# SSM layer of a two-layer decoder trunk: u exchanged inside SBUF, one order of loads for tables and GLU weights, gelu's table loaded earlier, gemvs moved out of the last stages, four gating buffers

## The chip, the cores and the metric

The kernel runs on one core of one Trainium2 chip. The core has a matrix engine (TensorE, PE in the profile), a vector engine (VectorE, DVE), a scalar engine (ScalarE, ACT), a general engine (GpSimd, POOL), a synchronisation engine (SyncE, SP) that here issues most DMAs, and 16 DMA engines that all queues share. Each engine works through its own list of instructions in order; an instruction waits until the semaphores it names have reached their values. The metric is the device time of one execution in microseconds (us).

## The reference

The whole computation is a decoder trunk of two layers on one sequence of 512 tokens and 1024 channels, all in float32. Layer 0 mixes tokens by stick-breaking attention, layer 1 by a complex diagonal state-space model (SSM) with a gated linear unit; a gated feed-forward layer with a short causal convolution follows each. The change is in the SSM:

```python
def s5_ssm(h, w_in, a_re, a_im, log_dt, b_re, b_im, c_re, c_im, d_skip, w_glu, b_glu, w_o):
    b, s, d = h.shape
    u = h @ w_in
    ug = u.reshape(b, s, N_GROUPS, SSM_GROUP)            # 64 groups of 16 channels
    lam = lax.complex(a_re, a_im)
    dt = jnp.exp(log_dt)[:, None]
    lam_bar = jnp.exp(lam * dt)
    b_bar = ((lam_bar - 1) / lam)[..., None] * lax.complex(b_re, b_im)
    bu = jnp.einsum('gph,bsgh->bsgp', b_bar, ug)
    # states: x[t] = lam_bar * x[t-1] + bu[t], 64 complex states for each group
    _, states = lax.associative_scan(combine, (a_seq, bu), axis=1)
    y = jnp.einsum('ghp,bsgp->bsgh', c_mat, states).real.reshape(b, s, d)
    z = jax.nn.gelu(y + d_skip * u)
    g = z * jax.nn.sigmoid(z @ w_glu + b_glu)
    return g @ w_o
```

## The kernel before

Tokens lie along the free axis and channels along the 128 partitions, so x is eight tiles of 128x512. A product of float32 values is made of three matmuls (`mm3`, L167): each operand is split into a rounded part (h) and a remainder (l), and TensorE adds hh, hl and lh. A weight is loaded by SP into a raw buffer, ScalarE makes the h part, DVE the l part (`load_w`, L145).

The SSM layer works on eight blocks of 128 channels. The 512 tokens are 64 chunks of 8. For block bi:

- `u_out` (L1149): the product u = h w_in is copied from PSUM by ScalarE into `ut` (two buffers), reordered by place in the chunk. ScalarE's queue writes it to DRAM (`sU`, L1153), SP's queue reads it back (L1155) in the form that the scan needs: a partition holds one of a group's 16 channels at one of the 8 places in the chunk. `u` has four buffers.
- `st_scan` (L1168): TensorE makes `pv` from u and table `pB`; DVE rotates it with table `pR`, scans over the 64 chunks (L1192) and rotates back; ScalarE copies the states into `st`. ScalarE first copies the decay rates into `rho` (L1172).
- `st_out` (L1205): TensorE makes `py`, first sixteen matmuls of u with table `pT` (inside a chunk), then sixteen of `st` with table `pC` (from the chunks before); ScalarE copies it to `yn`.
- `st_tr` (L1217): four transposes by TensorE into `pz`, then ScalarE's gelu gives z (L1223). Gelu lies in another function table of ScalarE than what ran before it, so an ACT_TABLE_LOAD stands ahead of its first use.
- `glu_units`, `glu_w` (L1239, L1246): z times the GLU weights. Five of the eight output tiles are accumulated block by block (weights `wglk`), the other three at the end (weights `wgl`). Sigmoid, the gating product and its split follow (L1298 to L1305), into `sg`, `gzH`, `gzL`; then the out-projection (weights `wos`) adds to x, tile by tile.

The loop over s_ from 2 to 9 (L1261) runs these as a pipeline: in stage s_ stand py of block s_-2, pv of block s_, some dense matmuls, pz of block s_-2 and more dense matmuls. The tables B, R, T and C of every block were computed earlier and lie in DRAM (`sB`, `sR`, `sT`, `sC`); each has two buffers in SBUF, and its load for block bi waits until block bi-2 has read its own.

TensorE's order is written out (`pe_pin`, pinned matmuls); a scheduler orders the rest by its own estimate. `follow("P", ...)` chains DMAs on SP's queue in program order. `behind_head` keeps work behind given instructions.

The gemvs (`gemv_step`, L191) are single steps of adaLN's modulation: a 512 KB tile of `w_modT` is loaded by SP into `wg` (two buffers) and reduced by DVE in one instruction (L196). `bg(n)` puts the next n of them at a place in the program.

Every DMA that SP or ScalarE issues signals its end on one of eight completion counters (DMAHW0 to DMAHW7 below; POOL's are DMASW0 to DMASW7). They are dealt out in turn over both queues, and a DMA that takes a counter waits until the DMA that had it last has landed.

## Time and profile before

| | before |
|---|---|
| time, median of 3 runs | 1194.81 us (1194.74 to 1198.65) |
| time of the profiled execution | 1194.65 us |
| its span | 1192.7 us |
| mean clock granted to TensorE | 0.991 |
| SSM layer in the span, roughly | 640 to 830 us |
| DMA, hardware queue of SP (q1) | 83026 packets, 205.76 MB, 53.9% of 16 engines |
| DMA, hardware queue of ScalarE (q10) | 8320 packets, 2.10 MB, 0.8% |
| DMA, software queue of POOL (q0) | 576 packets, 2.10 MB, 0.5% |

The span is the time from the first to the last instruction in the profile. A row of a timeline gives start and duration in us, the engine (SPq and ACTq are DMAs being issued by SP and ScalarE), the line, the operation, what it writes <- what it reads, and how often it stands in a row (x2). In brackets stands how long the engine had been idle before it, and what ended that. In the chain of waits a row is start, duration, and what the time went to. A row of a window lists its length and then, for PE, PEld, DVE, ACT and POOL, the busy time and the number of instructions, and at the end the clock, the share of the DMA engines and GB/s. A row of waits gives the line, what it waited for, the sum in us, how often, and the longest.

### The profile page before, as it was taken

To read this page: it belongs to the slowest core of one execution; us is meant where nothing else is said; L and a number is where in the kernel's file an instruction comes from. 1 tells how busy PE (TensorE), PEld (TensorE's weight loads), DVE (VectorE), ACT (ScalarE), POOL (GpSimd) and SP (SyncE) were. 2 spreads that over 40 slices of the span, in tenths; PEclk is the share of its full clock that TensorE was granted. 3 is DMA by queue.
4 is the path that set the end of the run, shared out by engine and by line. 5 is a ranking of instruction groups with operands and counts; after the bars stand their busy time and mean duration, and the time that the engine had idled before them with its cause. 6 is when DMAs were issued, how large, how long until landed. Compare 5 with 4: busy or idle time off the path is not lost.

```text
span 1192.7 us, 16459 instructions
## 1 busy us (share of the span) xinstructions
PE 1168.8 (98%) x6218; PEld 964.4 (81%) x6218; DVE 885.8 (74%) x1312; ACT 563.7 (47%) x893; POOL 270.4 (23%) x245
## 2 busy tenths in 40 slices
PE   8999999999999999989999999999999999999997
PEld 6887677699787878768889887879888888888887
DVE  6978988565999489888868598787598467744555
ACT  6756667456443134413336577646554134422443
POOL 1000000000298899998710000000000000000003
PEclk8999999999999999989999999999999999999999
DMA  8875653231348567778755598762166437442222
GB/s 301 316 262 165 203 179 109 90 121 54 89 142 273 177 215 222 207 233 294 247 153 182 182 322 288 246 224 77 53 216 225 124 118 188 153 124 71 83 76 71
DMA packets 92002, 211.00 MB, mean 177 GB/s; under 512 B 19602, under 2 KB 37906, under 8 KB 91923
## 3 DMA queue, kind: packets, MB, share of 16 engines
q1 hardware_dynamic: 83026, 205.76, 53.9%
q10 hardware_dynamic: 8320, 2.10, 0.8%
q0 software_dynamic: 576, 2.10, 0.5%
q8 instruction: 48, 0.79, 0.3%
q14 instruction: 32, 0.25, 0.1%
HBM read 188.68 MB, written 21.24 MB: 176 GB/s over the span
## 4 chain that ended last, share of the span: by engine, by line
PE 70%; POOL 8%; DVE 8%; DMA 7%; ACT 3%; issue 2%; SPq 1%; POOLq 0%; ACTq 0%; DVEq 0%
PE up L169 9%; PE up L172 9%; PE up L173 9%; PE dn L172 5%; PE dn L169 5%; PE dn L173 5%; PE o L772 2%; DVE ca L459 1%; PE t L754 1%; PE k L169 1%; PE q L169 1%; PE wo L169 1%; PE q L172 1%; PE q L173 1%; PE wo L173 1%
## 5 line engine op out<-in xcount | busy, mean ns | idle before, releaser
L173 PE MATMUL up<-hH,up_l 128*128 128x512 f32 x640 | 249.3, 390 | 1.1 <-DVE up_l L164 1.1
L169 PE MATMUL up<-hH,up_h 128*128 128x512 f32 x640 | 249.5, 390 | 0.0
L172 PE MATMUL up<-hL,up_h 128*128 128x512 f32 x640 | 249.3, 390 | 0.0
L459 DVE SCALAR_TENSOR_TENSOR ca<-up,small,ca 128x511 f32<-128x511 f32 (+1 forms) x176 | 131.4, 746 | 84.2 <-ACT ca L457 81.4
L196 DVE SCALAR_TENSOR_TENSOR wg<-wg,cact 128x1024 f32<-128x1024 f32 x96 | 122.8, 1294 | 40.1 <-DMA wg<-in_w_modT_dram 39.9
L172 PE MATMUL dn<-gL,dn_h 128*128 128x512 f32 (+1 forms) x394 | 145.9, 370 | 3.4 <-DVE gL L474 3.4
L169 PE MATMUL dn<-gH,dn_h 128*128 128x512 f32 (+1 forms) x394 | 146.3, 372 | 2.1 <-ACT gH L473 2.1
L173 PE MATMUL dn<-gH,dn_l 128*128 128x512 f32 (+1 forms) x394 | 145.7, 370 | 0.0
L173 PEld LDWEIGHTS up<-hH,up_l 128*128 128x128 f32 x640 | 120.1, 188 | 26.9 <-DVE up_l L164 2.0
L169 PEld LDWEIGHTS up<-hH,up_h 128*128 128x128 f32 x640 | 120.1, 188 | 26.0 <-issue 1.2
L172 PEld LDWEIGHTS up<-hL,up_h 128*128 128x128 f32 x640 | 120.1, 188 | 24.4
L1368 POOL TENSOR_SCALAR xa<-x,Anorm_out 128x256 f32<-128x256 f32 x7 | 5.7, 815 | 573.7 <-ACT dn_h L163 558.9
L163 ACT ACTIVATE up_h<-up_r 128x1024 fp32r<-128x1024 f32 x80 | 84.2, 1053 | 104.7 <-PE dn L172 48.0
L164 DVE TENSOR_TENSOR up_l<-up_r,up_h 128x1024 fp32r<-128x1024 f32 x80 | 121.9, 1524 | 10.1 <-ACT up_h L163 9.2
L457 ACT ACTIVATE ca<-up,small 128x512 f32<-128x512 f32 x88 | 67.7, 770 | 90.3 <-PE up L173 90.3
L172 PEld LDWEIGHTS dn<-gL,dn_h 128*128 128x128 f32 x394 | 75.1, 191 | 16.3 <-DVE gL L474 4.0
L169 PEld LDWEIGHTS dn<-gH,dn_h 128*128 128x128 f32 x394 | 75.0, 190 | 15.9 <-ACT gH L473 3.0
L173 PEld LDWEIGHTS dn<-gH,dn_l 128*128 128x128 f32 x394 | 75.0, 190 | 12.4
L353 DVE SCALAR_TENSOR_TENSOR x<-dn,mod,x 128x512 f32<-128x512 f32 (+1 forms) x55 | 37.3, 679 | 61.6 <-PE dn L173 61.6
L163 ACT ACTIVATE dn_h<-dn_r 128x1024 fp32r<-128x1024 f32 (+1 forms) x48 | 46.7, 981 | 55.9 <-PE dn L172 28.0
L466 ACT ACTIVATE ca<-ca 128x512 f32<-128x512 f32 x44 | 27.8, 632 | 91.7 <-DVE ca L459 89.9
L164 DVE TENSOR_TENSOR dn_l<-dn_r,dn_h 128x1024 fp32r<-128x1024 f32 (+1 forms) x48 | 62.8, 1308 | 8.3 <-ACT dn_h L163 8.1
(324 smaller groups left out, 2352.2 us busy)
## 6 DMA issues: line engine op xcount, KB each, us to landing
wg<-in_w_modT_dram SPq DMA_DIRECT2D x96, 512.0 KB
up_r<-in_w_up_dram SPq DMA_DIRECT2D x80, 512.0 KB
dn_r<-in_w_down_dram SPq DMA_DIRECT2D x32, 512.0 KB
wgs<-in_w_modT_dram SPq DMA_DIRECT2D x16, 512.0 KB
dn_r<-in_w_down_dram SPq DMA_DIRECT2D x16, 384.0 KB
wv_r<-in_w_v_dram SPq DMA_DIRECT2D x8, 512.0 KB
wk_r<-in_w_qk_dram SPq DMA_DIRECT2D x8, 512.0 KB
wq_r<-in_w_qk_dram SPq DMA_DIRECT2D x8, 512.0 KB
```

Source lines behind the costliest of these rows:

```text
L163: order("S", lambda: S.activation(wh[:, :n], raw[:, :n], AF.Copy))
L164: pin["split"] = order("V", lambda: V.tensor_tensor(wl[:, :n], raw[:, :n], wh[:, :n].bitcast(F32), ALU.subtract))
L169: ins = PE.matmul(ps, ah, bh, start=start, stop=False)
L172: PE.matmul(ps, ah, bl, start=False, stop=False)
L173: PE.matmul(ps, al, bh, start=False, stop=stop)
L196: mul = lambda: V.scalar_tensor_tensor(w, w, 1.0, cact, ALU.mult, ALU.mult, accum_out=raw[:, col:col + 1])
L353: add = lambda: V.scalar_tensor_tensor(xs, pv, gate, xs, ALU.mult, ALU.add)
L457: follow("S", lambda: S.activation(ca, ps, AF.Identity, bias=small[:, cb:cb + 1], scale=tapw[2]))
L459: follow("V", lambda: V.scalar_tensor_tensor(ca[:, q:], ps[:, :T - q], tapw[2 - q], ca[:, q:], ALU.mult, ALU.add))
L466: follow("S", lambda: S.activation(cg, cg, AF.Silu))
L754: ins = PE.transpose(pt[:, c:c + P], wts[pr][h2][i][:, j * P:(j + 1) * P], ident)
L772: ins = PE.matmul(po[pr][h2 * HD:(h2 + 1) * HD, j * P:], vn[:, j, hd:hd + HD], src, start=j == 0, stop=j == 3)
```

## The change

- u goes from `ut` straight to `u` inside SBUF: eight DMAs a block, one for each place in the chunk, each 32 KB in pieces of 256 bytes. Blocks 0 to 3 issue them on ScalarE's queue, blocks 4 to 7 on POOL's. `sU` and its DMAs are gone.
- One ACTIVATE with gelu on a single column (`warm`) stands behind the first four `u_out`, so that the table load comes there.
- The loads of the four tables and of `wglk` are chained on SP in one order by stage: R of the next block, T and C of this one, B of the one after next, then `wglk` (`load_tab`, `glu_load`). Before, B and R were loaded together, and `wglk` was not chained. The weights `win4` to `win7` are loaded in calls of their own.
- `bg(4)` stands ahead of block 0's scan; at stage 9 and after the last GLU units there is none any more; the out-projection has up to two gemvs behind each tile instead of one.
- `sg` has four buffers instead of two.

```diff
--- before.py
+++ after.py
@@ -142,7 +142,7 @@
         return line[eng]
 
 
-    def load_w(src, n=D, name="w", own=None, lined=False):
+    def load_w(src, n=D, name="w", own=None, lined=False, chain=False):
         raw = wp.tile([P, D], F32, tag="wraw", bufs=3, name=name + "_r")
         if isinstance(own, list):
 
@@ -158,7 +158,8 @@
         else:
             wh = wp.tile([P, D], F32R, tag="wH", bufs=NW, name=name + "_h")
             wl = wp.tile([P, D], F32R, tag="wL", bufs=NW, name=name + "_l")
-        pin["load"] = SP.dma_start(raw[:, :n], src)
+        fetch = lambda: SP.dma_start(raw[:, :n], src)
+        pin["load"] = follow("P", fetch) if chain else fetch()
         order = follow if lined else lambda eng, fn: fn()
         order("S", lambda: S.activation(wh[:, :n], raw[:, :n], AF.Copy))
         pin["split"] = order("V", lambda: V.tensor_tensor(wl[:, :n], raw[:, :n], wh[:, :n].bitcast(F32), ALU.subtract))
@@ -1099,7 +1100,6 @@
         return step
 
 
-    sU = dram.tile([8, CH, P, NC], F32, tag="sU", name="sU")
     sV = dram.tile([T + 1, D], F32, tag="sV", name="sV")
 
     def ssm(R):
@@ -1113,24 +1113,20 @@
             with ExitStack() as sc:
                 tp = sc.enter_context(tc.tile_pool(name="sst", bufs=1, reuse_waits="tile"))
 
-                def load_scan(bi):
-                    d = blk[bi]
-                    d["B"] = tp.tile([P, 2, 512], F32, tag="pB", bufs=2, name="pB")
-                    d["R"] = tp.tile([P, 2, 256], F32, tag="pR", bufs=2, name="pR")
-                    for g, src in (("B", sB), ("R", sR)):
-                        follow("P", lambda: SP.dma_start(d[g].rearrange("p r n -> p (r n)"), src[bi].rearrange("p r n -> p (r n)")))
-
-                def load_out(bi):
-                    d = blk[bi]
-                    d["T"] = tp.tile([P, 8, P], F32, tag="pT", bufs=2, name="pT")
-                    d["C"] = tp.tile([P, 8, P], F32, tag="pC", bufs=2, name="pC")
-                    for g, src in (("T", sT), ("C", sC)):
-                        follow("P", lambda: SP.dma_start(d[g].rearrange("p r n -> p (r n)"), src[bi].rearrange("p r n -> p (r n)")))
+                SRC = {"B": (sB, [P, 2, 512]), "R": (sR, [P, 2, 256]), "T": (sT, [P, 8, P]), "C": (sC, [P, 8, P])}
+
+
+                def load_tab(bi, which):
+                    for g in which:
+                        src, shape = SRC[g]
+                        if bi < 8:
+                            t = blk[bi][g] = tp.tile(shape, F32, tag="p" + g, bufs=2, name="p" + g)
+                            follow("P", lambda: SP.dma_start(t.rearrange("p r n -> p (r n)"), src[bi].rearrange("p r n -> p (r n)")))
 
                 for bi in range(2):
-                    load_scan(bi)
+                    load_tab(bi, "BR")
                 for bi in range(2):
-                    load_out(bi)
+                    load_tab(bi, "TC")
                 hx, ws = pin["hw"]
                 hd = [(ws[bi], bank(name=f"u{bi}")) for bi in range(4)]
                 head_mm(R, h, a, b, hd)
@@ -1150,14 +1146,17 @@
                     d = blk[bi]
                     ut = sp.tile([P, CH, NC], F32, tag="ut", bufs=2, name="ut")
                     S.activation(ut, ps.rearrange("p (c j) -> p j c", j=CH), AF.Copy)
-                    S.dma_start(sU[bi].rearrange("j p c -> p j c"), ut)
                     u = d["u"] = sp.tile([P, 8, NC], F32, tag="u", bufs=NU, name="u")
-                    pin["u"] = SP.dma_start(u.rearrange("p g c -> p (g c)"), sU[bi].rearrange("j (h g) c -> h j (g c)", g=8))
+
+                    for j in range(CH):
+                        (S if bi < NU else G).dma_start(u[j:P:CH], ut[:, j, :])
 
                 for bi in range(4):
                     u_out(bi, hd[bi][1])
-                u_loads = pin["u"]
                 bg(2)
+
+                warm = np_.tile([P, 64], F32, tag="warm", bufs=1, name="warm")[:, 0:1]
+                pe_pin(S.activation(warm, ones[:, 0:1], AF.Gelu_apprx_tanh))
 
                 rhos = [sp.tile([P, 4, NC], F32, tag=f"rho{q}", name=f"rho{q}") for q in range(2)]
                 sts = [sp.tile([P, 8, NC], F32, tag=f"st{q}", name=f"st{q}") for q in range(2)]
@@ -1224,10 +1223,14 @@
                                          pz[i * 64:i * 64 + 64].rearrange("p (a g c) -> p a g c", a=4, g=2)[:, :, g2, :], AF.Gelu_apprx_tanh)
                     tap(f"z{bi}", zf[bi])
 
+                uw = {}
+
+                def u_load(bi):
+                    with behind_head(pin["head"][HEADW[bi - 4]]):
+                        uw[bi] = load_w(I["w_in"][bi * P:(bi + 1) * P, :], name=f"win{bi}")
+
                 def u_units(bi):
-                    with behind_head(pin["head"][HEADW[bi - 4]]):
-                        w = load_w(I["w_in"][bi * P:(bi + 1) * P, :], name=f"win{bi}")
-                    ps = bank(name=f"u{bi}")
+                    w, ps = uw[bi], bank(name=f"u{bi}")
 
                     def unit(k):
                         mm3(ps, wk(w, k), (h[0][k], h[1][k]), k == 0, k == KD - 1, True)
@@ -1237,23 +1240,35 @@
                     dense.extend(lambda k=k: unit(k) for k in range(KD))
 
                 def glu_units(k):
-                    with behind_head([u_loads]):
-                        w = load_w(I["w_gluk"][k * P:(k + 1) * P, :], n=NGLU * P, name=f"wglk{k}")
+                    w = gw_[k]
                     S.activation(zh[0][k], zf[k], AF.Copy)
                     V.tensor_tensor(zh[1][k], zf[k], zh[0][k].bitcast(F32), ALU.subtract)
                     dense.extend(lambda mt=mt: mm3(gb[mt], wk(w, mt), (zh[0][k], zh[1][k]), k == 0, k == KD - 1, True) for mt in range(NGLU))
 
+
+                gw_ = {}
+
+                def glu_load(k):
+                    if k < KD:
+                        gw_[k] = load_w(I["w_gluk"][k * P:(k + 1) * P, :], n=NGLU * P, name=f"wglk{k}", chain=True)
+
                 def glu_w(mt):
                     return load_w(I["w_glu"][(mt - NGLU) * P:(mt - NGLU + 1) * P, :], name=f"wgl{mt}")
 
+                for bi in range(4, 8):
+                    u_load(bi)
                 u_units(4)
                 u_units(5)
+                with behind_head([pin["split"]]):
+                    bg(4, False)
                 run(UPRE)
                 st_scan(0)
-                load_scan(2)
+                load_tab(2, "BR")
                 u_units(6)
                 run(USTG[0])
                 st_scan(1)
+                load_tab(3, "B")
+                glu_load(0)
                 u_units(7)
                 run(USTG[1])
                 pz = bank(name="pz")
@@ -1262,10 +1277,10 @@
                     st_out(s_ - 2)
                     if s_ < 8:
                         st_scan(s_)
-                    if s_ + 1 < 8:
-                        load_scan(s_ + 1)
-                    if s_ < 8:
-                        load_out(s_)
+                        load_tab(s_ + 1, "R")
+                        load_tab(s_, "TC")
+                        load_tab(s_ + 2, "B")
+                    glu_load(s_ - 1)
                     if s_ > 2:
                         if s_ == 3:
                             zh = new_h()
@@ -1273,12 +1288,14 @@
                         glu_units(s_ - 3)
                     run(2)
                     st_tr(s_ - 2)
-                    if s_ >= 8:
+                    if s_ == 8:
                         with behind_head([pin["comb"]]):
                             bg(4, False)
                     run(100)
 
-                gw, g5 = glu_w(NGLU), bank(aux, name=f"glu{NGLU}")
+                with behind_head([line["P"]]):
+                    gw = glu_w(NGLU)
+                g5 = bank(aux, name=f"glu{NGLU}")
                 for k in range(KD - 1):
                     mm3(g5, wk(gw, k), (zh[0][k], zh[1][k]), k == 0, False, True)
                 glu_units(KD - 1)
@@ -1295,7 +1312,7 @@
                     ps = bank(name=f"glu{mt}")
                     for k in range(KD):
                         mm3(ps, wk(w, k), (zh[0][k], zh[1][k]), k == 0, k == KD - 1)
-                sg = gp.tile([P, T], F32, tag="sg", bufs=2, name="sgl")
+                sg = gp.tile([P, T], F32, tag="sg", bufs=4, name="sgl")
                 S.activation(sg, ps, AF.Sigmoid, bias=sm("b_glu", mt, 1))
                 V.tensor_tensor(sg, sg, zf[mt], ALU.mult)
                 gh = gp.tile([P, T], F32R, tag=f"gzH{mt}", name=f"gzH{mt}")
@@ -1303,10 +1320,8 @@
                 S.activation(gh, sg, AF.Copy)
                 V.tensor_tensor(gl, sg, gh.bitcast(F32), ALU.subtract)
                 gz.append((gh, gl))
-                if mt >= len(gb):
-                    bg(2)
             acc2 = new_acc()
-            R = out_proj(lambda mt: I["w_os"][mt * P:(mt + 1) * P, :], gz, mcol(1, 2, 0), acc2, "wos", perm=True, after=lambda: bg(min(1, sum(q[0] is not None for q in bgq) - 24)),
+            R = out_proj(lambda mt: I["w_os"][mt * P:(mt + 1) * P, :], gz, mcol(1, 2, 0), acc2, "wos", perm=True, after=lambda: bg(min(2, sum(q[0] is not None for q in bgq) - 24)),
                          head=([up_src(1, q, s) for q in range(2) for s in range(2)], "uph"))
         return R
 
```

On ScalarE, before, around yn of block 0 (`py_6560`). `ut` with `u_6465` is block 6's, `st_6357` and `st_6358` are the states of blocks 0 and 1, `rho_6356` is block 1's:

```order
L1153 DMA sU<-ut 128x8x64 [waits Activation_49]
L1202 ACTIVATE st_6357<-m_6445 64x4x63 [waits DVE_49]
L1202 ACTIVATE st_6357<-m_6445 64x4x63
L1202 ACTIVATE st_6357<-m_6445 64x4x63 [waits DVE_49]
L1202 ACTIVATE st_6357<-m_6445 64x4x63
L163 ACTIVATE wglk_h<-wglk_r 128x640 [waits DMAHW0_49]
L163 ACTIVATE wglk_h<-wglk_r 128x640 [waits DMAHW1_49]
L163 ACTIVATE wglk_h<-wglk_r 128x640 [waits DMAHW2_49]
L1172 ACTIVATE rho_6356<-decay 128x4x63 [waits DVE_49]
L1152 ACTIVATE ut<-u_6465 128x512 [waits DMAHW5_49,PE_49]
L1153 DMA sU<-ut 128x8x64 [waits Activation_49]
L1215 ACTIVATE yn<-py_6560 128x4x8x16 [waits PE_49]
```

The same place now, from the last three of block 3's eight DMAs to yn of block 0 (`py_6623`). `u_6412` is block 4's, `st_6383` block 1's:

```order
L1152 DMA u<-ut 16x8x64 [waits DMAHW7_49]
L1152 DMA u<-ut 16x8x64 [waits DMAHW1_49]
L1152 DMA u<-ut 16x8x64 [waits DMAHW2_49]
L1159 ACT_TABLE_LOAD
L1159 ACTIVATE warm<-ones 128x1
L1148 ACTIVATE ut<-u_6412 128x512 [waits DMAHW3_49,PE_49]
L1201 ACTIVATE st_6383<-m_6571 64x4x63 [waits DVE_49]
L1201 ACTIVATE st_6383<-m_6571 64x4x63
L1201 ACTIVATE st_6383<-m_6571 64x4x63 [waits DVE_49]
L1201 ACTIVATE st_6383<-m_6571 64x4x63
L164 ACTIVATE wglk_h<-wglk_r 128x640 [waits DMAHW3_49]
L1214 ACTIVATE yn<-py_6623 128x4x8x16 [waits PE_49]
```

The table load has moved ahead of yn, and so have block 3's eight DMAs, whose sixth and seventh wait for counters 7 and 1. The loads that had these counters last are on SP's queue, where the order at that place now is (pB of blocks 2 and 3, wg76 and wg77, pR of block 2, then pR of block 3 and pT of block 2, which have counters 7 and 1):

```order
L1124 DMA pB<-sB 128x1024 [waits DMAHW6_49,PE_49]
L196 DMA wg_7267<-in_w_modT_dram 128x1024 [waits DMAHW0_49,DVE_49]
L1124 DMA pR<-sR 128x512 [waits DMAHW5_49,DVE_49]
L1124 DMA pB<-sB 128x1024 [waits DMAHW1_49,PE_49]
L161 DMA wglk_r<-in_w_gluk_dram 128x640 [waits DMAHW3_49,Activation_49]
L1124 DMA pR<-sR 128x512 [waits DMAHW7_49,DVE_49]
L1124 DMA pT<-sT 128x1024 [waits DMAHW1_49,PE_49]
L1124 DMA pC<-sC 128x1024 [waits DMAHW3_49,PE_49]
L1124 DMA pB<-sB 128x1024 [waits DMAHW6_49,PE_49]
```

Before, SP issued these loads between the DMAs that read u back, and the load of pC that follows pT of block 5 waits for counter 2, which a DMA of ScalarE had (block 7's `sU<-ut`):

```order
L1121 DMA pR<-sR 128x512 [waits DMAHW7_49,DVE_49]
L1155 DMA u<-sU 128x1x512 [waits DMAHW0_49,PE_49]
L1128 DMA pT<-sT 128x1024 [waits DMAHW1_49]
L1128 DMA pC<-sC 128x1024 [waits DMAHW2_49,PE_49]
L161 DMA wglk_r<-in_w_gluk_dram 128x640 [waits DMAHW3_49,DVE_49]
L1121 DMA pB<-sB 128x1024 [waits DMAHW4_49,PE_49]
```

The DMAs of u are gone from SP's queue, and pR of the next block now stands ahead of pT and pC.

## The prediction

> **What bounds the kernel now.** The page's first part comes first. Then TensorE's own timeline, cut to the SSM layer (about 640 to 830 us), to the rows that carry an idle time in brackets and what ended it.
>
> ```profile
> PE 1168.8 (98%) x6218; PEld 964.4 (81%) x6218; DVE 885.8 (74%) x1312; ACT 563.7 (47%) x893; POOL 270.4 (23%) x245
> ```
> ```profile
> 707.67 0.66 PE L1220 MATMUL pz<-consts,yn 128*128 128x128 f32 x4 [0.59 <-ACT yn L1215]
> 727.29 1.15 PE L1146 MATMUL pv<-u,pB 128*64 128x64 f32 x32 [1.12 <-DVE wgl_l L164]
> 734.86 1.15 PE L1146 MATMUL pv<-u,pB 128*64 128x64 f32 x32 [0.42 <-DVE m L1197]
> 744.85 0.66 PE L1220 MATMUL pz<-consts,yn 128*128 128x128 f32 x4 [1.24 <-ACT yn L1215]
> 777.56 0.49 PE L169 MATMUL wos<-gzH,wos_h 128*128 128x512 f32 x1 [0.19 <-ACT gzH L1303]
> 778.93 0.50 PE L172 MATMUL wos<-gzL,wos_h 128*128 128x512 f32 x1 [0.88 <-DVE gzL L1304]
> ```
>
> TensorE is the bound. Where the change works it loses 0.59 + 1.12 + 0.42 + 1.24 + 0.19 + 0.88 = 4.4 us in six gaps. The matmuls and their order are untouched, so 4.4 us (0.4%) is the most that can be won here. Nothing caps a loss: an operand that comes late on this engine is paid in full.
>
> Next, the waits of the SP queue between 705 and 730 us, SP's timeline there, one ScalarE row, the DVE rows that follow, and the chain that ended last.
>
> ```profile
> SPq L1128 <- DMA sU<-ut: 8.2, 1, 8.2
> ```
> ```profile
> 712.05 0.58 SPq L1128 DMA_DIRECT2D pT<-sT  x1
> 720.85 0.32 SPq L1128 DMA_DIRECT2D pC<-sC  x1
> ...
> 721.73 0.38 SPq L1121 DMA_DIRECT2D pB<-sB  x1
> 722.21 0.38 SPq L1121 DMA_DIRECT2D pR<-sR  x1
> ```
> ```profile
> 705.46 0.37 ACTq L1153 DMA_DIRECT2D sU<-ut  x1
> ```
> ```profile
> 728.80 0.69 DVE L1188 TENSOR_TENSOR m<-pv,pR 128x512 f32<-128x512 f32 x1 [1.52 <-DMA pR<-sR]
> ```
> ```profile
> 722.21 6.50 DMA pR<-sR
> ```
>
> SP stands still from 712.63 to 720.85. The next load, pC, shares one of eight completion counters with the DMA of u that ScalarE issued at 705.46, and a counter is taken again only when its last DMA has landed. So that DMA was in flight for some 15 us. The tables pB and pR go out at 721.73 and 722.21 instead of about 713, pR lands 6.50 us later, and the gaps at 727.29 and 734.86 follow.
>
> **The change part by part.** (1) *u without DRAM.* The DMA that held SP is gone, and with it those two gaps: 1.12 + 0.42 = 1.5 us won. But the same rule of counters now works on ScalarE's queue. Each of blocks 0 to 3 issues eight DMAs there instead of one. By the order of instructions, the sixth and seventh of block 3 take the counters of the loads of pR (block 3) and pT (block 2). Behind them in ScalarE's order stand gelu's table load, ut of block 4, four st copies, one wglk_h, and only then yn of block 0, which TensorE's first pz transposes need. When is that yn ready?
>
> ```profile
> 694.29 1.09 PE L1146 MATMUL py<-pT,u 128*64 128x128 f32 x16
> 695.21 1.04 PE L1146 MATMUL py<-pC,st 128*64 128x128 f32 x16
> ...
> 698.61 0.60 PE L1220 MATMUL pz<-consts,yn 128*128 128x128 f32 x4
> ```
> ```profile
> 684.03 0.69 DVE L1188 TENSOR_TENSOR m<-pv,pR 128x512 f32<-128x512 f32 x1 [6.76 <-PE pv L1146]
> ...
> 689.42 0.69 DVE L1188 TENSOR_TENSOR m<-pv,pR 128x512 f32<-128x512 f32 x1
> ```
> ```profile
> 695.08 0.58 ACT L1152 ACTIVATE ut<-u 128x512 f32<-128x512 f32 x1
> ...
> 696.30 0.60 ACT L1215 ACTIVATE yn<-py 128x512 f32<-128x512 f32 x1 [0.65 <-PE py L1146]
> 697.87 0.84 ACT L1202 ACTIVATE st<-m 64x252 f32<-64x252 f32 x2 [0.97 <-DVE m L1197]
> 698.74 0.74 ACT L163 ACTIVATE wglk_h<-wglk_r 128x640 fp32r<-128x640 f32 x1
> 699.50 0.85 ACT L1202 ACTIVATE st<-m 64x252 f32<-64x252 f32 x2
> 700.37 1.28 ACT L1223 ACT_TABLE_LOAD   x1
> ```
> ```profile
> 743.97 3.58 DMA wg<-in_w_modT_dram
> ```
> ```profile
> L1022 SPq DMA_DIRECT2D sT<-kz x64: 570/570/882, 453.4 to 611.7; - x64
> ```
>
> pT of block 2 goes into the buffer that py's first sixteen matmuls read, so it cannot be issued before they end at 695.2, and SP needs some 0.4 us for it: 695.6. A load of its size (512 KB, the wg row) lands in 3.58: 699.2. Only then go the seventh and eighth DMA, at 0.57 each (the nearest small shaped DMA, sT<-kz): 700.3. Then 1.28 for the table, 0.2 for its first use (an estimate), 0.58 ut, 0.84 + 0.85 st, 0.74 wglk_h, 0.60 yn: 705.4. In the kernel before, pz began at 698.61 without a wait, so TensorE stands **6.8 us**. Below: if no counter held ScalarE, block 3's eight DMAs could still not start before DVE is past block 1's scan (684.03 + 0.7 for part 2, a block of 5.39, and 3.7 into the next: about 694). At 0.37 each, as the sU row has it, they end at 697 and yn at 702.1: 3.5 us. Above: 6.50 for pT's landing, as pR had in a full queue, gives 9.7. I take 6.8, because few loads are ahead of pT at that point. The delay gives ScalarE time to catch up, so the gap of 0.59 before the second pz goes (-0.6).
>
> The Trainium skill (ScalarE: Activation LUTs, Rules for kernel authors) budgets about 2.7 us for a switch of table set. The row here says 1.28, and the row decides; by the page the stall would be 1.4 us longer.
>
> Blocks 4 to 7 issue 32 such DMAs on POOL. Every fourth u shares a buffer, so block 5's can start only when block 1's py has read its own.
>
> ```profile
> L992 POOL DMA_DIRECT2D sR<-tb x4: 769/782/932, 358.1 to 398.3; - x4
> ...
> DMA to landing us min/median/max: 3.4/3.5/4.3
> ```
> ```profile
> 702.59 1.09 PE L1146 MATMUL py<-pT,u 128*64 128x128 f32 x16
> ...
> 714.66 0.60 PE L1220 MATMUL pz<-consts,yn 128*128 128x128 f32 x4
> ```
>
> Those matmuls end at 703.5 + 6.8 = 710.4. Eight at 0.78 end at 716.6, the last lands at 720.1, ut of block 7 (which takes block 5's ut buffer and stands ahead of yn of block 2) ends at 720.7, that yn at 721.3. The third pz is due at 714.66 + 6.2 = 720.9: **0.5 us** lost. Ends: at 0.93 and 4.3 it is 2.5; if so small a transfer lands a microsecond sooner, nothing. In the half before, u of block 1 may land up to 1 us after its pv needs it; I value that at nothing, since block 0 has 4 us to spare.
>
> (2) *gemvs.* Four of the eight at stages 8 and 9 move to DVE's work ahead of block 0's scan. Two have their loads by then; the other two wait for a buffer and a load of 3.58, then run 1.22 each, which pushes the scan from 684.03 to about 684.7. Its followers have that much to spare, so 0. Four stay at stage 8, and the gap of 1.24 there is left as it is: 0, ends -1.2 (gone) and +1.2 (one gemv more). Without the two at each of the last GLU units, and with four gating buffers, gzH and gzL no longer queue: 0.19 + 0.88 = 1.1 won. Those four go behind the residual add of x0 in the out-projection, to the four that were there.
>
> ```profile
> 784.29 1.23 DVE L196 SCALAR_TENSOR_TENSOR wg<-wg,cact 128x1024 f32<-128x1024 f32 x1 [2.51 <-DMA wg<-in_w_modT_dram]
> ...
> 786.98 1.28 DVE L353 SCALAR_TENSOR_TENSOR x<-wos,mod,x 128x512 f32<-128x512 f32 x1
> ```
> ```profile
> 790.00:800.00 10.00, 10.00 (x46) 8.29 (x45) 10.00 (x13) 4.23 (x5) 0.00 (x0) 1.00 0.80 251
> ```
>
> DVE is full there, and four more gemvs behind x0 are 4 x 1.22 = 4.9 us. But x0 no longer stands behind them, and starts some 4 us sooner than 786.98, when DVE had waited 2.51 for a gemv's load. I take 0, up to 2.3 lost if the extra gemvs reach the norm's statistics.
>
> (3) *Table and GLU loads in one order.* What they can win, the two gaps, is in part 1.
>
> **Sum:** 6.8 - 0.6 + 0.5 - 1.5 - 1.1 = +4.1 us. The profiled execution took 1194.65 us (span 1192.7 and 1.95 around it), 0.16 below the median, so 1194.65 + 4.1 = **1198.8 us**.
>
> **The rivals.** *A, the queue of ScalarE is cheaper than I think* (loads land in time, a DMA costs 0.37): the stall is 3.5 and the gains stand: 3.5 - 0.6 - 1.5 - 1.1 = +0.3, 1195.0. For it speaks the sU row; against it that DVE's scan sets the same floor, so no case with this order reaches the 4.4 us of gain. Were ScalarE not held at all, it would be 1190.3; by the order it is.
>
> *B, slower: POOL cannot issue fast enough.* ut has two buffers, so ut of block 6 waits for block 4's POOL DMAs and stands ahead of yn of block 1, due at 707.08 + 6.8 = 713.9. Block 4's ut ends at 702.5; with p us per issue that yn is ready at 702.5 + 8p + 3.5 + 1.2. It decides from p = 0.85. At p = 1.13 (0.78 and half of a 0.69 DVE instruction) TensorE loses 2.3 there and 2.0 again a block later, against 0.5 in my sum: 1202.6. At 1.47 (behind a whole one) it loses 5.0 + 4.8: 1208. What speaks for it is how POOL's work fares beside DVE:
>
> ```profile
> 387.64 1.91 POOL L870 TENSOR_TENSOR tt<-tb,co 128x512 f32<-128x512 f32 x1
> 389.52 1.04 POOL L871 TENSOR_TENSOR tt<-tb,si 128x512 f32<-128x512 f32 x1
> ```
>
> The same operation takes 1.04 or 1.91. Against it, the four DMA issues in that busy stretch all lie between 0.77 and 0.93. The Trainium skill (SBUF: State Buffer, "SBUF: two separate sides") says that DVE and GpSimd take a shared port in turn, whole instructions at a time, and that descriptors of a POOL DMA cannot be written meanwhile. By that rule B holds wherever DVE uses both ports; the four issues don't show it.
>
> **How the numbers follow.** 0.5% (6 us) is about what a measurement of this kernel tells from no change. My forecast 0.62 (its own range 1196.5 to 1202), A 0.15, B 0.20, and 0.03 that something wins beyond the gaps. Slower by over 0.5%, above 1200.8: B, and a third of the forecast's share for a late pT or the 2.3 us of the out-projection: 0.20 + 0.21, 0.41. Faster by over 0.5%: 0.03. Within: 0.56. The range goes from A's 1195 to 1206, inside B.
>
> **What would show it.** On TensorE one gap of 5 to 8 us before the first pz, ended by yn, and nothing above 1 us at the pv of 727 and 735; ScalarE's queue waiting for pT<-sT at about 699; SP with no wait of 8 us; wos without a gap. If the first pz comes without a wait, my order of causes is wrong and the time is near 1190. If the second and third pz wait for yn behind ut, B holds.

## The result, and the profile after

The changed kernel takes **1222.92 us** (median of 4, 1220.25 to 1225.74) against 1194.81 (median of 4): a ratio of **1.0237, 95% interval 1.0214 to 1.0261**. It is slower by 28 us, far outside the range of 1195 to 1206. The profiled execution took 1225.74 us, span 1223.9, which is 31.2 more span than before.

First part of the page, then all of TensorE's waits from 640 to 870 us (line, what was waited for, sum, times, longest):

```profile
PE 1177.9 (96%) x6218; PEld 969.3 (79%) x6218; DVE 878.7 (72%) x1312; ACT 562.6 (46%) x894; POOL 285.6 (23%) x277
```
```profile
PE pz L1219 <- ACT yn L1214: 10.6, 3, 8.0
PE glu L170 <- ACT ut L1148: 9.0, 1, 9.0
PE pv L1142 <- DMA wg<-in_w_modT_dram: 4.4, 1, 4.4
PE glu L173 <- DVE hL L1245: 1.3, 2, 0.8
PE glu L170 <- ACT hH L1244: 0.6, 1, 0.6
PE u L173 <- DVE hL L320: 0.2, 1, 0.2
```

The same 6218 matmuls are busy 1177.9 us instead of 1168.8, and they wait 26.1 us in this layer where the same view of the kernel before adds up to 4.6. So there are two losses: **21.5 us more standing still, and matmuls that are slower**. TensorE's timeline shows the four large stops, and the windows (length, busy time of PE, PEld, DVE, ACT, POOL, clock, DMA share, GB/s) show what comes behind them:

```profile
694.87 1.52 PE L1142 MATMUL pv<-u,pB 128*64 128x64 f32 x32 [4.45 <-DMA wg<-in_w_modT_dram]
...
714.97 1.11 PE L1219 MATMUL pz<-consts,yn 128*128 128x128 f32 x4 [7.99 <-ACT yn L1214]
...
736.34 0.79 PE L170 MATMUL glu<-hH,wglk_h 128*128 128x512 f32 x1 [8.99 <-ACT ut L1148]
...
752.71 0.66 PE L1219 MATMUL pz<-consts,yn 128*128 128x128 f32 x4 [2.44 <-ACT yn L1214]
```
```profile
696.00:698.00 2.00, 2.00 (x12) 1.59 (x9) 1.54 (x3) 0.89 (x2) 0.00 (x0) 0.50 0.47 74
...
716.00:718.00 2.00, 2.00 (x6) 1.53 (x5) 0.83 (x1) 1.93 (x4) 0.88 (x2) 0.50 0.20 53
...
738.00:740.00 2.00, 2.00 (x22) 2.00 (x24) 0.00 (x0) 0.00 (x0) 0.00 (x0) 0.54 0.00 0
```

In these windows TensorE is busy all the time and its granted clock is half or little more (0.50, 0.50, 0.54). Four transposes that took 0.60 us before take 1.11 behind the stop at 714.97. Busy time times (1 - clock), summed over all windows of 2 us from 640 to 880 us, gives **7.2 us** of work lost to the clock. Before, no window of this layer has a clock below 1.

The account: 21.5 of stops and 7.2 of clock are 28.7, and the SSM layer begins 2.15 later (its first matmul that waits, u, starts at 653.47 instead of 651.32, behind work that the change doesn't touch). Together that is 30.9 of the 31.2.

Where the stops come from is seen on ScalarE, in its timeline:

```profile
677.57 10.85 ACTq L1152 DMA_DIRECT2D u<-ut  x14
688.82 0.60 ACT L1148 ACTIVATE ut<-u 128x512 f32<-128x512 f32 x1 [10.66 <-DMA wg<-in_w_modT_dram]
...
699.79 10.30 ACTq L1152 DMA_DIRECT2D u<-ut  x8
710.12 1.28 ACT L1159 ACT_TABLE_LOAD   x1 [9.98 <-DMA pB<-sB]
...
714.33 0.58 ACT L1214 ACTIVATE yn<-py 128x512 f32<-128x512 f32 x1
...
733.36 0.74 ACT L164 ACTIVATE wglk_h<-wglk_r 128x640 fp32r<-128x640 f32 x1 [4.86 <-DMA wglk_r<-in_w_gluk_dram]
...
735.69 0.60 ACT L1148 ACTIVATE ut<-u 128x512 f32<-128x512 f32 x1
```

- **694.87, pv of block 1 (4.45).** In the fourteen DMAs from 677.57, two wait for completion counters of `wg` loads. Those two loads have to wait in turn until the gemvs now ahead of the scan have read their buffer. The two waits on the counters take 0.3 and 1.1 us of this stop. The larger part is the landing: the last DMA of u of block 1 goes out at 687.80, beside the `wg` and pB loads, and lands at 694.68, 6.9 later, where the first and last of block 0 took 4.4 and 3.8. pv starts 0.2 after that. (The row names a wg load that ended at about the same time.)
- **714.97, the first pz (7.99).** The eight DMAs of block 3 take 10.30: the sixth goes at 703.86, the seventh only at 708.90, 0.02 after the pT load issued at 703.62 had landed (708.88). These two waits on counters are 0.9 and 4.5 of the 10.30, and the issuing itself is the rest. This is the chain that was predicted; the row names pB, which landed later. Table load, ut, wglk_h and yn follow, until 714.9.
- **736.34, GLU tile 5 of block 0 (8.99).** Its PSUM bank held the u of block 7, and is free when ScalarE has copied that u into `ut` at 735.69. Two things hold this copy.

```profile
722.68 4.16 POOL L1152 DMA_DIRECT2D u<-ut  x8 [5.81 <-issue]
```
```profile
L1152 ACTq DMA_DIRECT2D u<-ut x32: 539/609/1060, 676.3 to 709.5; - x32
L1152 POOL DMA_DIRECT2D u<-ut x32: 527/527/572, 712.7 to 751.1; - x32
...
DMA to landing us min/median/max: 1.7/6.2/7.2
```
```profile
724.39 0.40 SPq L161 DMA_DIRECT2D wglk_r<-in_w_gluk_dram  x1
```

The first is the pair of `ut` buffers: block 7's is block 5's, whose eight POOL DMAs go out from 722.68, when py of block 1 has freed a `u`, and whose last lands at 733.1. The second is `wglk_h` of block 2, which stands ahead of that copy in ScalarE's order: its load left SP only at 724.39, behind three table loads, and the ACT row above waits for it until 733.36. The two end within 0.3 us of each other, so this trace can't say which of them alone would have made the stop. In the kernel before, the write to DRAM needed no `u` buffer, so no bank hung on py, and block 7's copy ran at about 704.8.

- **752.71 (2.44)** and the rest (2.1): yn and the GLU operands are late behind further weights. ScalarE waits 12.4 us in all for `wglk_r`.

### The profile page after: what moved, and what is told of

Same layout as the page of the kernel before. It is cut to its first block, busy times and chain, and to the rows that moved or that the text cites. A ratio compares the mean times of both kernels' runs of the same rounds, so it can differ in the third digit from the quotient of the medians.

```text
span 1223.9 us, 16556 instructions
## 1 busy us (share of the span) xinstructions
PE 1177.9 (96%) x6218; PEld 969.3 (79%) x6218; DVE 878.7 (72%) x1312; ACT 562.6 (46%) x894; POOL 285.6 (23%) x277
## 4 chain that ended last, share of the span: by engine, by line
PE 75%; DVE 10%; DMA 7%; ACT 3%; issue 2%; POOL 1%; SPq 1%; POOLq 0%; ACTq 0%; DVEq 0%
PE up L170 9%; PE up L173 9%; PE up L174 9%; PE dn L173 6%; PE dn L170 6%; PE dn L174 6%; DVE ca L460 2%; DMA up_r<-in_w_up_dram 2%; DMA wg<-in_w_modT_dram 2%; DMA wglk_r<-in_w_gluk_dram 2%; PE o L773 2%; DVE up_l L165 2%; PE t L755 1%; PE wos L170 1%; PE wos L174 1%
## 5 line engine op out<-in xcount | busy, mean ns | idle before, releaser
L165 DVE TENSOR_TENSOR up_l<-up_r,up_h 128x1024 fp32r<-128x1024 f32 x80 | 119.9, 1498 | 11.6 <-ACT up_h L164 10.7
L174 PEld LDWEIGHTS dn<-gH,dn_l 128*128 128x128 f32 x394 | 74.9, 190 | 12.2
```

The lines of the kernel that those rows point to most:

```text
L165: pin["split"] = order("V", lambda: V.tensor_tensor(wl[:, :n], raw[:, :n], wh[:, :n].bitcast(F32), ALU.subtract))
L174: PE.matmul(ps, al, bh, start=False, stop=stop)
```

## The experiments

The theories, by the letters that the expectations use: **C**, ScalarE's queue is held by completion counters of loads; **G**, the gemvs ahead of the scan make that worse, since their loads come late; **U**, two `ut` buffers tie the bank of u of block 7 to the DMAs of block 5; **W**, GLU weights land late behind the tables; **K**, every stop is followed by matmuls at half clock. Each of U and W could explain the stop of 8.99 alone. The kernel before ran beside each group: 1189.61 (once) beside the first four, 1195.68 (median of 16) beside the next four, 1194.39 (of 7) beside the three after, 1193.30 (of 13) beside the last.

**e1: four ut buffers** (those of blocks 6 and 7 lie in another pool).

```diff
-ut = sp.tile([P, CH, NC], F32, tag="ut", bufs=2, name="ut")
+ut = sp.tile([P, CH, NC], F32, tag="ut", bufs=2, name="ut") if bi < 6 else np_.tile([P, T], F32, tag="nt1", bufs=2, name="ut").rearrange("p (j c) -> p j c", j=CH)
```

> The kernel after, but ut of blocks 6 and 7 lie in two buffers of their own, so that they no longer wait for POOL's DMAs of blocks 4 and 5 to land. Theory U (the 9.0 us stop of TensorE at the fifth GLU tile of block 0 is the PSUM bank of u of block 7, which ScalarE frees only when POOL's DMAs of block 5 have landed): that stop goes, and with it about 2 us of half clock behind it; pv of block 1 (4.4) and the first pz (8.0) stay: about 1211 us (1208 to 1214). Rival W (the stop is the late load of wglk of block 2, ahead of ut of block 7 in ScalarE's order): a stop of 5 us or more stays behind that load, 1217 to 1224.

One run: 1217.79, above the 1208 to 1214 that was expected under U. The stop of 8.99 is gone. At the same place a smaller one appears, with the GLU weights ahead of it on ScalarE (TensorE's timeline, then ScalarE's):

```profile
735.94 1.11 PE L1219 MATMUL pz<-consts,yn 128*128 128x128 f32 x4 [3.97 <-ACT yn L1214]
```
```profile
720.66 0.60 ACT L1148 ACTIVATE ut<-u 128x512 f32<-128x512 f32 x1 [0.69 <-PE u L174]
...
732.96 0.74 ACT L164 ACTIVATE wglk_h<-wglk_r 128x640 fp32r<-128x640 f32 x1 [4.93 <-DMA wglk_r<-in_w_gluk_dram]
```

The first of these rows is the copy of block 7's u. It now stands ahead of `wglk_h` of block 2 in ScalarE's order, where it stood behind it, so this edit frees the copy of U and of W at once: it shows that with two more buffers the stop goes, and not which of the two made it. The late weight is still there and stops a pz instead, so the edit pays only in part.

**e2: GLU weights loaded ahead of the stage's tables.**

```diff
                     if s_ < 8:
                         st_scan(s_)
+                        glu_load(s_ - 1)
                         load_tab(s_ + 1, "R")
                         load_tab(s_, "TC")
                         load_tab(s_ + 2, "B")
-                    glu_load(s_ - 1)
+                    else:
+                        glu_load(s_ - 1)
```

> The kernel after, but each stage loads the GLU weight of its block ahead of the tables R, T, C and B on SP's chain, not behind them. Theory U: wglk of block 2 lands early, but ut of block 7 still waits for POOL's DMAs of block 5, so the stop at the fifth GLU tile stays at 7 us or more: 1219 to 1225. Rival W: the stop goes, with the half clock behind it: about 1211.

One run: 1222.10. The stop stays at 7.99, ended by ut. ScalarE's timeline:

```profile
730.49 0.74 ACT L164 ACTIVATE wglk_h<-wglk_r 128x640 fp32r<-128x640 f32 x1 [3.87 <-DMA wglk_r<-in_w_gluk_dram]
...
732.82 0.60 ACT L1148 ACTIVATE ut<-u 128x512 f32<-128x512 f32 x1
```

Block 2's weight is early here: its load leaves SP at 705.29. But block 3's, which leaves at 722.52, has taken its place ahead of that copy, and it lands at 730.5, as the last of block 5's DMAs does (730.4). So this run doesn't part U from W either. U by itself is seen in e12 below, where the weights aren't chained, with stops of 2.5 and 2.3; what it would cost alone in the kernel after stays open.

**e4: all of u on POOL's queue.**

```diff
-                        (S if bi < NU else G).dma_start(u[j:P:CH], ut[:, j, :])
+                        G.dma_start(u[j:P:CH], ut[:, j, :])
```

> The kernel after, but all eight blocks send u by POOL's queue, none by ScalarE's. Theory C (the stops at pv of block 1, 4.4 us, and at the first pz, 8.0 us, come from ScalarE's DMAs that wait for the counters of loads on SP): both go, with some 3 to 4 us of half clock; but ut of blocks 6 and 7 wait for POOL's DMAs of 4 and 5 and stand behind wglk of block 2, so the fourth and fifth GLU tile of block 0 stop TensorE for 6 to 10 us: 1204 to 1211. Rival D (pieces of 256 bytes land late on any queue): pv of block 1 still stops by 3 us or more: above 1214.

One run: 1211.61, a little above the 1204 to 1211 that was expected under C. TensorE's timeline has no stop at pv of block 1, and 0.88 instead of 7.99 at the first pz; U's place, with fewer stops ahead of it, comes at 716:

```profile
700.53 0.66 PE L1219 MATMUL pz<-consts,yn 128*128 128x128 f32 x4 [0.88 <-ACT yn L1214]
...
712.04 0.66 PE L1219 MATMUL pz<-consts,yn 128*128 128x128 f32 x4 [2.99 <-ACT yn L1214]
...
716.54 0.79 PE L170 MATMUL glu<-hH,wglk_h 128*128 128x512 f32 x1 [3.15 <-ACT ut L1148]
```

So the two early stops come from u on ScalarE's queue, as C has it. This edit takes two things off ScalarE at once, the waits on counters and the issuing at about 0.6 us each. How they share a stop can only be read from the rows (0.3 and 1.1 of the first stop, 0.9 and 4.5 ahead of the second are counters); no run parts them.

**e5: gemvs back where they were in stages 8 and 9.**

```diff
-                with behind_head([pin["split"]]):
-                    bg(4, False)
...
-                    if s_ == 8:
+                    if s_ >= 8:
```

> The kernel after, but with the four gemvs ahead of block 0's scan put back to stages 8 and 9. Theory G (u of block 1 came late because two of its DMAs waited for the counters of the loads of wg74 and wg75, which wait for DVE's gemvs): pv of block 1 no longer stops (4.4 us and 1.5 us of half clock less); the stops at the first pz (7 to 9) and the fifth GLU tile (8 to 10) stay: 1215 to 1219. Rival: ScalarE's DMAs come late anyway, pv of block 1 stops by 3 us or more, 1221 to 1225.

One run: 1215.52. TensorE's timeline, then two rows of the chain of waits:

```profile
687.00 1.15 PE L1142 MATMUL pv<-u,pB 128*64 128x64 f32 x32 [0.32 <-DMA u<-ut]
...
705.80 1.11 PE L1219 MATMUL pz<-consts,yn 128*128 128x128 f32 x4 [8.24 <-ACT yn L1214]
...
727.64 0.80 PE L170 MATMUL glu<-hH,wglk_h 128*128 128x512 f32 x1 [9.02 <-ACT ut L1148]
```
```profile
693.95 5.74 DMA u<-ut
...
699.71 0.54 ACTq L1152
```

The first stop falls from 4.45 to 0.32 and the other two stand. So the stop at pv takes both G and u on ScalarE's queue, and either one undone removes it. In the chain, block 3's sixth DMA goes out at 699.71, when ScalarE's own DMA of 693.95, which had its counter before, has landed. Here it is no load that holds the queue ahead of the first pz, so C as worded is too narrow: a queue is held by whatever DMA had the counter last, its own ones too.

**e3: e1 and e2 together.**

> The kernel after with the edits of e1_ut4 and e2_glu together. Theory U+W (once ut of blocks 6 and 7 are free of POOL's DMAs, what is left of the later stops is ScalarE waiting for late GLU weights): neither the 9.0 us stop of the kernel after nor the 4.0 us one of e1_ut4 is there; pv of block 1 (3 to 4) and the first pz (7 to 8) stay; 1206 to 1212. Rival (the later stops come from POOL's DMAs holding the scan): stops of 3 us or more behind 725 us stay, 1214 or more.

One run: 1215.61. The stop at GLU tile 5 is gone, but 3.58 and 3.26 remain at later pz, where e1 had 3.97 and 2.68. The expectation (1206 to 1212) missed, and the time is in the rival's range; but ScalarE waits 10.0 us for `wglk_r`, so it is the weights and not POOL's DMAs. Putting them first in their stage doesn't bring them in time.

**e6: e1, e2 and e4 together.**

> The kernel after with all of u on POOL, ut of blocks 6 and 7 in buffers of their own, and the GLU weights ahead of the tables. If the three causes (counters on ScalarE's queue, ut that waits for POOL, GLU weights behind the tables) are the whole loss: no stop of TensorE over 2.5 us in the SSM layer, no half clock, ratio to before 0.997 to 1.006. If one is missing: 1.01 or more.

1206.88 (median of 7), ratio 1.0100 (1.0072 to 1.0129). Stops of 3.63, 4.29 and 2.95 are left, all of them pz behind yn. ScalarE's waits from 690 to 748 us:

```profile
ACT wglk_h L164 <- DMA wglk_r<-in_w_gluk_dram: 12.9, 6, 5.3
```

With C and U out of the way, the GLU weights are as late as ever (12.4 before this edit). In a chain it doesn't help to stand first in a stage, since the loads of the stage before wait for buffers ahead of it. A cause was missing from my list: the chain itself.

**e9: a stop alone.** The kernel before with twelve copies of yn of block 0 onto itself, which leave its values as they are.

```diff
+                    for _ in range(12 if bi == 0 else 0):
+                        S.activation(yn, yn, AF.Copy)
```

> The kernel before with twelve extra copies in place of yn of block 0 on ScalarE (the values stay), which only make the first pz late. Theory K (a stop of some us lets TensorE's clock fall to half, also where nothing else is changed): one stop of 8 to 11 us, granted clock 0.5 for 3 to 5 us of work behind it, and the time grows by the stop and 1.5 to 2.5 us more. Rival (the half clock belongs to the DMAs on ScalarE and POOL): clock 1.00 behind the stop, and the time grows by the stop alone.

One run: 1208.09, 12.4 more than the kernel before. TensorE's timeline and windows:

```profile
712.70 1.12 PE L1222 MATMUL pz<-consts,yn 128*128 128x128 f32 x4 [10.55 <-ACT yn L1217]
```
```profile
714.00:716.00 2.00, 2.00 (x6) 1.56 (x5) 0.00 (x0) 1.93 (x5) 0.00 (x0) 0.50 0.00 0
...
718.00:720.00 2.00, 2.00 (x25) 1.56 (x25) 0.44 (x1) 1.19 (x2) 0.00 (x0) 1.00 0.00 0
```

Six matmuls in a window at clock 0.50, twenty-five at 1.00. The stop of 10.55 and 2.3 of clock are 12.9. But the other waits of this layer fall from 4.6 to 1.6 behind it, so the net is 9.9, against 12.4 measured in a single run, which can be off by that much. The clock rows don't hang on it: half clock comes behind this stop with no DMA and nothing else of the change in it, as K has it (not behind every stop, as the last section shows).

**e11: the kernel before with only the new order of table and GLU loads** (`load_tab` and `glu_load` as in the change, and the last GLU weights behind the chain; the loads of win stay inside `u_units`).

```diff
-                def load_scan(bi):
-                def load_out(bi):
+                def load_tab(bi, which):
...
-                    with behind_head([u_loads]):
-                        w = load_w(I["w_gluk"][k * P:(k + 1) * P, :], n=NGLU * P, name=f"wglk{k}")
+                    w = gw_[k]
...
+                        gw_[k] = load_w(I["w_gluk"][k * P:(k + 1) * P, :], n=NGLU * P, name=f"wglk{k}", chain=True)
```

> The kernel before with the new order of loads alone (tables by stage, GLU weights chained behind them, the last GLU weights behind the chain); u goes by DRAM as before. If the order costs by itself: ScalarE waits for GLU weights by 8 us or more in sum, TensorE stops by 3 us or more at GLU tiles or pz, ratio to before 1.003 to 1.012. If it is harmless without the exchange inside SBUF: 0.997 to 1.002.

1207.59 (median of 4), ratio 1.0111 (1.0088 to 1.0134). This kernel takes 13 us more than the one before, with u still going through DRAM. TensorE's largest waits from 640 to 870 us and SP's timeline:

```profile
PE u L170 <- ACT win_h L164: 4.7, 1, 4.7
PE pz L1217 <- ACT yn L1212: 4.3, 3, 3.6
PE glu L173 <- DVE hL L1239: 2.3, 2, 1.9
```
```profile
688.78 0.33 SPq L1125 DMA_DIRECT2D pB<-sB  x1
689.15 0.43 SPq L161 DMA_DIRECT2D wglk_r<-in_w_gluk_dram  x1
689.99 0.33 SPq L161 DMA_DIRECT2D win_r<-in_w_in_dram  x1
```

The 4.7 and the half clock behind it (2.7 of the 4.3 below) are special to this kernel: `win7` stands on SP behind the chained loads, and the change itself asks for it earlier. So some 6 us of the 13 are left for the order as the change has it. The 4.3 and 2.3 are the late GLU weights again, without C, G or U.

**e10: u on POOL, four ut buffers, GLU weights not chained** (loaded in `glu_units`, as before, and held until block 7's u was issued).

```diff
-                        (S if bi < NU else G).dma_start(u[j:P:CH], ut[:, j, :])
+                        pin["ulast"] = G.dma_start(u[j:P:CH], ut[:, j, :])
...
+                pin["u"] = pin["ulast"]
...
-                    w = gw_[k]
+                    with behind_head([pin["u"]]):
+                        w = load_w(I["w_gluk"][k * P:(k + 1) * P, :], n=NGLU * P, name=f"wglk{k}")
```

> The kernel after with all of u on POOL, ut of blocks 6 and 7 in buffers of their own, and the GLU weights loaded as before (not chained behind the tables). If the chain of loads is what was left in e6_pool_ut4_glu (three stops of 3.6, 4.3 and 3.0 us): no stop over 1.5 us in the SSM layer, no half clock, ratio to before 0.995 to 1.001. Rival (what was left belongs to POOL's late DMAs): stops of 3 us or more stay, ratio 1.006 or more.

1201.81 (median of 4), ratio 1.0069 (1.0046 to 1.0092). TensorE's largest waits from 640 to 880 us:

```profile
PE glu L170 <- ACT hH L1246: 3.5, 1, 3.5
PE pz L1220 <- ACT yn L1215: 3.1, 1, 3.1
```

The two later pz stops of e6 are gone. Two others are left, more than expected: the first pz, and a GLU tile at 745 where ScalarE had waited 4.6 us for a `wgl` weight. The ratio lies in the rival's range (late DMAs of POOL); e13 below settles that. The intervals of e6 and e10 overlap, so it is the stops that differ clearly, and not the times.

**e12: e10 with the two ut buffers of the change.**

> As e10_pool_ut4_oldglu, but with the two ut buffers that the kernel after has. Theory U by itself (ut of block 7 waits for POOL's DMAs of block 5, which wait for py of block 1, and holds a PSUM bank that block 0's fifth GLU tile needs): one stop of 4 to 7 us there, half clock behind it, 5 to 9 us more than e10_pool_ut4_oldglu. Rival: without the late GLU weights two buffers are enough, no stop over 1.5 us.

One run: 1207.75, 5.9 above e10. TensorE's largest waits from 640 to 880 us:

```profile
PE glu L170 <- ACT ut L1148: 4.8, 2, 2.5
PE pz L1220 <- ACT yn L1215: 3.8, 2, 2.8
PE pv L1142 <- DMA u<-ut: 2.9, 1, 2.9
```

The wait for ut is back, which confirms U from the other side, though in two stops of 2.5 and 2.3 where one of 4 to 7 was expected. Waits and clock together are 2.8 above e10's; the rest of the 5.9 lies within what a single run can be off by.

**e13: e10, and the gemvs in stages 8 and 9 and the first wgl load as before.** Of the change there remain the exchange of u (all on POOL), the order of the tables, the early table load of gelu, the gemvs in the out-projection and four gating buffers.

```diff
-                with behind_head([pin["split"]]):
-                    bg(4, False)
...
-                    if s_ == 8:
+                    if s_ >= 8:
...
-                with behind_head([line["P"]]):
-                    gw = glu_w(NGLU)
+                gw = glu_w(NGLU)
```

> As e10_pool_ut4_oldglu, but with the gemvs back at stages 8 and 9 and the load of the last GLU weights as before: what is left of the change is u inside SBUF (all on POOL, ut of blocks 6 and 7 in buffers of their own), gelu's table ahead, the tables' order R, T, C, B, four gating buffers and gemvs out of the GLU tail. If the stops of 3.1 us (first pz) and 3.5 us (GLU at 745) in e10 come from the gemvs ahead of the scan and from the last GLU loads behind the chain: no stop over 1.5 us, no half clock, ratio to before 0.994 to 1.000. Rival (the exchange by POOL is itself too late): the first pz still stops by 2.5 us or more, ratio 1.003 or more.

1194.24 (median of 10) against 1193.30, ratio **0.9998 (0.9977 to 1.0019)**. All of TensorE's waits from 640 to 880 us:

```profile
PE pz L1220 <- ACT yn L1215: 0.7, 2, 0.4
PE u L173 <- DVE hL L320: 0.2, 1, 0.2
```

So POOL's DMAs weren't what was left in e10. The exchange inside SBUF harms nothing that could be measured once neither ScalarE nor two `ut` buffers carry it, and it brings nothing that could be measured, though the six gaps of the prediction are gone or under half a microsecond. Which of the last two edits removed the stops of e10 was not tried apart.

**e8: the kernel before with two small edits**: the writes of u to DRAM of blocks 4 to 7 from POOL's queue, and four sg buffers.

```diff
-                    S.dma_start(sU[bi].rearrange("j p c -> p j c"), ut)
+                    (S if bi < NU else G).dma_start(sU[bi].rearrange("j p c -> p j c"), ut)
...
-                sg = gp.tile([P, T], F32, tag="sg", bufs=2, name="sgl")
+                sg = gp.tile([P, T], F32, tag="sg", bufs=4, name="sgl")
```

> The kernel before with two edits: blocks 4 to 7 write u to DRAM by POOL's queue, not ScalarE's (so that SP no longer shares a counter with that write), and four gating buffers. By the prediction's own step on SP's wait of 8.2 us: that wait and the gaps of 1.1 and 0.4 go, 1 us less in the GLU tail: ratio 0.997 to 0.999. Rival (the write on POOL lands late too, SP waits for it in its order): SP still waits 4 us or more, ratio 0.999 to 1.004.

1192.00 (median of 10) against 1195.68, ratio **0.997 (0.995 to 0.999)**, the only variant whose interval lies below 1. TensorE's waits from 640 to 880 us:

```profile
PE pz L1220 <- ACT yn L1215: 0.5, 1, 0.5
PE u L172 <- DVE hL L319: 0.2, 1, 0.2
```

It takes SP's wait of 8.2 us away at its root: these DMAs leave the counters that the loads use. The gain, 3.7, is about the 4.6 us that the layer waits before, less 0.7. Its two edits were not tried apart.

All runs side by side, each by its profiled execution: TensorE's waits from 640 to 880 us, the work lost to the clock as above, and the time less both.

| kernel | waits | clock | time of it | rest |
|---|---|---|---|---|
| before | 4.6 | 0 | 1194.65 | 1190.1 |
| after | 26.1 | 7.2 | 1225.74 | 1192.4 |
| e1 | 20.3 | 5.1 | 1217.79 | 1192.4 |
| e2 | 23.4 | 7.1 | 1222.10 | 1191.6 |
| e3 | 19.1 | 6.3 | 1215.61 | 1190.2 |
| e4 | 12.5 | 5.3 | 1211.61 | 1193.8 |
| e5 | 20.8 | 6.4 | 1215.52 | 1188.3 |
| e6 | 12.7 | 3.0 | 1210.91 | 1195.2 |
| e8 | 0.7 | 0 | 1190.62 | 1189.9 |
| e9 | 12.2 | 2.3 | 1208.09 | 1193.6 |
| e10 | 7.6 | 4.2 | 1200.51 | 1188.7 |
| e11 | 11.7 | 4.3 | 1206.35 | 1190.3 |
| e12 | 11.7 | 2.9 | 1207.75 | 1193.2 |
| e13 | 0.9 | 0 | 1193.21 | 1192.3 |

The rest stays between 1188.3 and 1195.2 while the time moves by 35 us. Within that spread of 7 us, which is what a single run can't resolve, the time of every variant is its stops in this one layer and their clock.

## Why the prediction was wrong, step by step

The mechanism that it put first was right; the sum was wrong because it priced one large stop where there are four, and none of the clock.

| step | predicted | in the trace |
|---|---|---|
| first pz, ScalarE's queue held until pT landed | 6.8 | 8.0 |
| u of block 1 "may land up to 1 us late", valued at nothing | 0 | 4.45 |
| third pz, behind ut of block 7 | 0.5 | no stop at pz; 8.99 at GLU tile 5, by the same ut and a late `wglk_h` |
| gap of 0.59; SP's wait and its two gaps; gzH and gzL | -0.6 -1.5 -1.1 | all gone; SP stands 11.6 elsewhere, behind a late py |
| order of loads: "what they can win, the two gaps" | nothing lost | 2.44 at a later pz, 1.9 at GLU operands |
| half clock behind stops | not in the sum | 7.2 |

1. **First pz.** Right in cause, and within its bounds (3.5 to 9.7). pT went out at 703.62 instead of 695.6, because the stop ahead had delayed everything, and landed in 5.3 instead of 3.58. A DMA took 0.61 to issue on ScalarE, where I had 0.57.
2. **u of block 1.** The step that failed is "I value that at nothing, since block 0 has 4 us to spare". I had applied the counter rule to block 3's DMAs only. The same rule holds block 1's: their counters belong to the `wg` loads that part 2 moved there. I also counted the gemvs as DVE time (0.7 on the scan; it measures 687.35, less the drift of 2.15, against 684.03: 1.2), and not their loads as something that ScalarE's queue would stand behind. e4 and e5 show that it takes both. Of the 4.45 the counters are 1.4; most of it is that the last DMA took 6.9 us to land beside those loads, where my rows for landing were 3.4 to 4.3.
3. **ut of block 7.** I followed this ut to yn of block 2 and found it nearly in time. I did not ask what the *copy itself* frees: a PSUM bank that a GLU tile needs. I also let its DMAs start at 710.4; they started at 722.68, pushed by the two stops ahead, and landed in up to 7.2 us instead of 3.4 to 4.3, in a full queue. e10 and e12 show the two buffers as a cause; in the kernel after, `wglk_h` of block 2 held the same copy just as long, and no run parts the two there.
4. **Order of loads.** I asked what it could win and not what it could hold up. In e11 it costs 13 us alone, about 7.4 of it (4.7 and 2.7 of half clock) by a load that only that kernel has late. e6 against e10 points to the chain of the GLU weights: without it ScalarE's waits for `wglk_r`, 12.9 us in e6, are gone, and the later pz stops with them.
5. **Clock.** "An operand that comes late on this engine is paid in full" was too low: it is paid in full, and then with 1 to 3 us more of slow work. I had rows for that in the kernel before, in another layer (TensorE's timeline and windows of before):

```profile
510.62 0.80 PE L172 MATMUL dn<-gL,dn_h 128*128 128x512 f32 x1 [2.72 <-DVE gL L474]
```
```profile
512.00:516.00 4.00, 4.00 (x25) 2.54 (x24) 4.00 (x5) 0.82 (x1) 4.00 (x2) 0.59 0.76 240
```

The Trainium skill (TensorE: Matmul & The Clock Gate, What's actually happening) says that the array falls to half clock after an idle window of about 3.4 us and returns after about as long of work, the windows running freely. The trace agrees in the length of the slow stretches: by the windows of 2 us the clock is at 0.50 for 3.4, 10.2, 10.2 and 3.4 us around the four stops, close to one or three times 3.4, of which 3.4 to 4.4 are work. The stops themselves need not be 3.4 long, as the last section shows.

6. **Rival B** is not borne out: POOL issues at 0.527 each, steadier and faster than 0.78, though DVE is busy beside it. The delay is in the landing, median 6.2. The out-projection lost nothing, as predicted, and the table load took 1.28 again. The sign "nothing above 1 us at the pv of 727 and 735" came true; for a stop at a GLU tile there was no sign, and U and W were no rival at all.

## What to carry to other kernels

When a transfer is moved to a queue, follow each completion counter that it takes to the DMA that had it last, for every block and not for the worst one alone, and follow every buffer and PSUM bank that the moved copy frees to its next user. Price a stop of the bounding engine above some 2 us with about 1 to 3 us of half clock behind it, and remember that one stop moves all later deadlines. Chain loads only with loads that free up at the same pace: in these runs weights that wait for nothing came late behind tables that wait for buffers.

## What the runs showed of the hardware

- Half clock comes behind shorter stops than one window, but not always. It followed single stops of 2.10 (e5), 2.44 (after) and 2.72 (before), and did not follow 2.68 (e1), 2.95 (e6) or 3.26 (e3). Behind every stop of 3.4 us or more it did. So from about 2 to 3.3 us it seems to be a matter of where the stop falls, which no run here tests.
- Thirty-two DMAs of 32 KB cost ScalarE 0.609 us each to issue, about 19.5 us for four blocks, where the single DMA of a block before took 0.37. The Trainium skill (DMA: Bandwidth & Descriptors, Rules for kernel authors) advises to join transfers under 64 KB, since they are mostly overhead; the trace agrees on ScalarE's side. On POOL the same DMAs cost 0.527, and in e13 they cost TensorE nothing.
- A DMA of 32 KB landed in 1.7 us at best and in 7.2 at worst, from POOL, in one kernel and one layer. Block 4's eight, with the DMA engines at a share of 0.20 from 716 to 718, landed in 1.7 to 1.8; block 5's, issued from 722.68 beside 1.86 MB of table and weight loads, in 3.6 to 7.2. Size is the same, so it is likely what else is in flight that decides.
- The time of the kernel before moved between 1188.8 and 1199.5 us over its executions in all groups, so only the runs with an interval bear a verdict of less than one per cent.
